# Two-layer mLSTM/HGRN2 encoder: the order of a few matmul pairs early in some weight-stationary chunks

## The chip, the cores and the metric

The kernel runs on one core of a Trainium2 chip. The metric is the device time of one execution in microseconds (us), as the median of several runs. All data is float32. Large products are made from two float32r parts of each factor, a high and a low one, of which three of the four cross products are kept.

## The reference, cut to what matters

The program is a trunk of two layers over 256 tokens of width 2048. Layer 0 mixes tokens with a bidirectional mLSTM, layer 1 with a bidirectional HGRN2. Each mixer is followed by a gated MLP with a convolution of width 3 (ConvGLU, inner width 5504), and a last norm closes it.

```python
D_MODEL = 2048; SEQ = 256; DEPTH = 2; D_FF = 5504

def conv_glu(hn, w_up, conv_w, conv_b, w_down):
    u = hn @ w_up
    a, v = jnp.split(u, 2, axis=-1)
    ...
    return (jax.nn.gelu(c, approximate=False) * v) @ w_down

def reference(...):
    ...
    h = x
    for layer in range(DEPTH):
        hn = rmsnorm(h, norm_mix_g[layer])
        mix = mlstm_mixer(...) if layer % 2 == 0 else hgrn_mixer(...)
        h = h + mix
        h = h + conv_glu(rmsnorm(h, norm_ffn_g[layer]), ffn_w_up[layer], ...)
    return rmsnorm(h, final_g)
```

Nearly all of the time goes into products of the 256 tokens with the weights: `mlstm_w_in`, `mlstm_w_out`, `hgrn_w_in`, `hgrn_w_out`, and in each layer `ffn_w_up` (2048 x 11008) and `ffn_w_down` (5504 x 2048). Each weight is read once, 447 MB in all.

## The kernel before, in words

**Chunks.** All products with weights are cut into chunks (class `Chunk`), which the function `stream` runs through in one long list. There are two main kinds.

- A chunk of kind "tm" keeps tiles of x stationary and streams 512 columns of weights. For each of the inner blocks k of 128 rows and each half t of the tokens it issues three products of 512 columns (lines 192 to 194): x high by weights high, x high by weights low, x low by weights high.
- A chunk of kind "fm" keeps 128 columns of weights stationary and streams the tokens. It has 256 output features, in two halves f. For each k (16 of them) and each f it issues a *pair*: the **high** product (line 202), the weights' high part by x high and x low side by side, 512 columns; and the **low** product (line 209), the weights' low part by x high alone, 256 columns. Both add into one PSUM bank, `ps[f]`. So an fm chunk is 32 pairs, in the order high, low, high, low. Pairs are counted from 0 in the code: pair 2k + f.

(A third kind, "first", is used once at the start.)

**Weights.** `split_weights` fetches the raw weights in pieces of 1 MB on the SyncE queue, and for every 1024 columns ScalarE casts the high part (`wh`, line 147) and VectorE subtracts to get the low part (`wl`, line 148). `LOOK = 3` such pieces are made ahead. For an fm chunk one piece holds four k, that is eight pairs.

**The list.** The mLSTM gives, for each of four pairs of heads, a v chunk (tm; for the first it is the "first" chunk), a q chunk and a k chunk (fm) and an o chunk (tm); then four output chunks (tm). HGRN2 gives, for each of four groups `qd` of heads, three fm chunks (i = 0, 1, 2), a v chunk (tm), three fm chunks (i = 3, 4, 5) and a g chunk (tm); then four output chunks (tm). Each ConvGLU runs in two parts, of 22 and 21 feature blocks: 22 fm chunks up and four tm chunks down, then 21 fm chunks up and four tm chunks down. So an fm chunk follows a tm chunk at each q chunk from the second on, at i = 0 and i = 3 of each group of HGRN2, and at the first up chunk of each part.

**Side work.** What else a layer does (attention heads, norms, transposes) is written as generators, which `side.tick` advances while the products are being issued; their TensorE instructions thus come to stand between pairs. The tile framework then schedules all instructions by its own estimate of times, so that the order on an engine can differ from the order in the text.

**Dummy transposes.** An fm chunk can have `turns`: behind the high product of pair 1 (k = 0, f = 1) it issues so many transposes of the identity into an auxiliary PSUM tile named `turns` (lines 203 to 206). Nothing reads the result. The second, third and fourth q chunk have 1, 2 and 2, and the first up chunk of the second part in each layer has 1: seven transposes in all.

Of the kernel before, what the change touches and what calls it, by code (L numbers as in the profile page):

```python
# [15 lines left out]
P = 128  # L16
T = 256
D = 2048
KT = D // P
# [36 lines left out]
def trunk_kernel(ctx, tc, xT, x_d, fg_d, pp_d, cst_d, w_first, w_aq, w_ak, w_av, w_ao, w_aout,  # L56
# [24 lines left out]
    def aux(name):  # L81
        return psa.tile([P, 512], F32, tag="aux", name=name)


    class Side:
        def __init__(self):
            self.now, self.jobs = 0.0, []
# [25 lines left out]
    side = Side()  # L113


    class Chunk:
        def __init__(self, kind, src, nk, x, done, before=None, last=False, turns=0):
            self.last, self.turns = last, turns
            self.kind, self.src, self.nk, self.x, self.done, self.before = kind, src, nk, x, done, before
            self.width = {"fm": 256, "tm": 512, "first": 512 + P}[kind]  # L120

# [30 lines left out]
    def stream(chunks):  # L152
        pieces = split_weights(chunks)
        ready = []

        def fetch():
            p = next(pieces, None)
            if p is not None:
                ready.append(p)

        for _ in range(LOOK):
            fetch()
        for ch in chunks:
            if ch.before:
                ch.before()
            ps = [psm.tile([P, 512], F32, tag="mm", name="mm") for _ in range(3 if ch.kind == "first" else 2)]
            k = 0
            while k < ch.nk:
                fetch()
                wh, wl, n = ready.pop(0)  # L170
                if ch.last and k + sum(p[2] for p in ready) + n == ch.nk:
                    pieces_, k0 = [(wh, wl, n)] + ready, k
                    for t in range(2):
                        k = k0
                        for wh, wl, n in pieces_:
                            for kk in range(n):
                                x, c = ch.x(k), slice(kk * 512, (kk + 1) * 512)
                                xh, xl = x[:, t * P:(t + 1) * P], x[:, T + t * P:T + (t + 1) * P]
                                pe.matmul(ps[t], xh, wh[:, c], start=False, stop=False)
                                pe.matmul(ps[t], xh, wl[:, c], start=False, stop=False)  # L180
                                pe.matmul(ps[t], xl, wh[:, c], start=False, stop=k == ch.nk - 1)
                                k += 1
                        ch.half(ps[t], t)
                    return
                for kk in range(n):
                    x = ch.x(k)
                    st, sp = k == 0, k == ch.nk - 1
                    if ch.kind != "fm":
                        c = slice(kk * 512, (kk + 1) * 512)
                        for t in range(2):  # L190
                            xh, xl = x[:, t * P:(t + 1) * P], x[:, T + t * P:T + (t + 1) * P]
                            pe.matmul(ps[t], xh, wh[:, c], start=st, stop=False)  # L192
                            pe.matmul(ps[t], xh, wl[:, c], start=False, stop=False)  # L193
                            pe.matmul(ps[t], xl, wh[:, c], start=False, stop=sp)  # L194
                        if ch.kind == "first":
                            pe.matmul(ps[2], wh[:, 512:512 + P], x, start=st, stop=False)
                            pe.matmul(ps[2][:, 0:T], wl[:, 512:512 + P], x[:, 0:T], start=False, stop=sp)
                        side.tick(1.3)
                    else:
                        for f in range(len(ps)):  # L200
                            c = kk * ch.width + f * P
                            pe.matmul(ps[f], wh[:, c:c + P], x, start=st, stop=False)  # L202
                            if f and k == 0 and ch.turns:
                                it = aux("turns")
                                for i in range(ch.turns):
                                    pe.transpose(it[:, i * P:(i + 1) * P], ident, ident)
                            if f:
                                side.tick(0.325 * len(ps))
                            pe.matmul(ps[f][:, 0:T], wl[:, c:c + P], x[:, 0:T], start=False, stop=sp)  # L209
                    k += 1  # L210
            ch.done(ps)

# [179 lines left out]
    def mlstm(norm, nxt):  # L392
# [151 lines left out]
        for pr in range(AH // 2):  # L544
            st = dict(pr=pr, y=[None, None], W=[None, None])

            def done_v(ps, st=st):
                Vh = box["mp"].tile([P, 2, 2, 258], F32R, tag="Vh", bufs=1, name="Vh")
                Vl = box["mp"].tile([P, 2, 2, 258], F32R, tag="Vl", bufs=1, name="Vl")
                for t in range(2):  # L550
                    act.copy(Vh[:, t, :, 256:258], pad[:, 0:4].rearrange("p (a b) -> p a b", a=2))
                    act.copy(Vl[:, t, :, 256:258], pad[:, 4:8].rearrange("p (a b) -> p a b", a=2))
                    v, sc = ps[t].rearrange("p (a b) -> p a b", a=2), norm.rc[:, t:t + 1]
                    act.activation(Vh[:, t, :, 0:256], v, AF.Copy, scale=sc)
                    dve.scalar_tensor_tensor(Vl[:, t, :, 0:256], v, sc, Vh[:, t, :, 0:256].bitcast(F32),
                                             ALU.mult, ALU.subtract)
                st["V"] = (Vh, Vl)

            def done_q(ps, st=st):
                st["q"] = [box["mp"].tile([P, T], F32, tag="q", bufs=2, name="q") for _ in range(2)]  # L560
                for j in range(2):
                    fm_scaled(ps[j], norm.R, st["q"][j], QSCALE)
                for j in range(2):
                    st["W"][j] = weights(2 * st["pr"] + j)

            def done_k(ps, st=st):
                st["k"] = [box["mp"].tile([P, T], F32, tag="k", bufs=2, name="k") for _ in range(2)]
                for j in range(2):
                    fm_scaled(ps[j], norm.R, st["k"][j])
                    side.push(head(st, j))  # L570

            def done_o(ps, st=st):
                sg = box["mp"].tile([P, 2, 512], F32, tag="sg", bufs=1, name="sg")
                for t in range(2):
                    act.activation(sg[:, t], ps[t], AF.Sigmoid, scale=norm.rc[:, t:t + 1])
                st["sg"] = sg
                side.push(finish(st))

            def done_first(ps, done_v=done_v):
                done_v(ps[0:2])  # L580
                gates(ps[2])
                for t in range(2):
                    pool.dma_start(hm[:, t], x_d[t])

            if pr == 0:
                chunks.append(Chunk("first", w_first, KT, first_x, done_first, begin))
            else:
                chunks.append(Chunk("tm", w_av[pr - 1], KT, norm.x, done_v))
            chunks.append(Chunk("fm", w_aq[pr], KT, norm.x, done_q, turns=(0, 1, 2, 2)[pr]))
            chunks.append(Chunk("fm", w_ak[pr], KT, norm.x, done_k))  # L590
            chunks.append(Chunk("tm", w_ao[pr], KT, norm.x, done_o))

# [13 lines left out]
    def hgrn(norm, nxt):  # L606
# [166 lines left out]
        for qd in range(BH // 4):  # L773
# [14 lines left out]
            for i in range(6):  # L788
                if i == 3:
                    chunks.append(Chunk("tm", w_bv[qd], KT, norm.x, done_v))  # L790
                def done_i(ps, i=i, qd=qd):
                    for f in range(2):
                        r = 2 * i + f
                        take(4 * qd + r // 3, r % 3, ps[f])
                chunks.append(Chunk("fm", w_bq[6 * qd + i], KT, norm.x, done_i, begin if not chunks else None))
            for j in range(4):
                heads[4 * qd + j]["qd"] = four
            chunks.append(Chunk("tm", w_bg[qd], KT, norm.x, done_g))
# [14 lines left out]
    def ffn(layer, norm, nxt):  # L813
# [30 lines left out]
        for part, (f0, nf) in enumerate(((0, FA), (FA, FB))):  # L844
            GT = []
            for i in range(nf):
                chunks.append(Chunk("fm", w_up[layer, f0 + i], KT, norm.x, done_up(f0 + i, i, GT),
                                    begin if f0 + i == 0 else None,
                                    turns=1 if part and i == 0 else 0))
            chunks += project(lambda c: w_down[layer, c][:, f0 * 512:(f0 + nf) * 512], nf,  # L850
                              lambda k, GT=GT: GT[k], nxt if part else None)
        return chunks, stack.close
# [108 lines left out]
```

## Time and profile before

| | |
|---|---|
| median of 3 runs | 2440.34 us (2439.63 to 2445.22) |
| the profiled execution | 2440.68 us, its span 2438.6 us |
| mean granted TensorE clock in it | 0.998 |
| VectorE, ScalarE, GpSimdE busy | 69%, 50%, 7% |
| memory read | 447.35 MB, 184 GB/s over the span |
| high products L202, low products L209 | 3776 each |
| products of the down and output projections and v, o, g chunks | 390 to 396 ns each by their groups |

The page lists groups of instructions as line, engine, operation, tiles out<-in, shapes, count, then busy time and mean duration in ns, then the idle time in front of them and what ended it. Matmuls overlap: a product's duration is longer than the distance to the next one's start, so paces are read from starts and counts, not from durations. In the timeline the columns are start and duration in us, engine, line and operation; equal neighbours are merged with their count. A window's row gives its length, each engine's busy time with the number of instructions, the granted clock, the DMA share and GB/s. In the trace of before, stretches are these (us from the start of the span):

| stretch | us |
|---|---|
| second, third, fourth q and k chunk of the mLSTM | 112.7 to 135, 185.7 to 208, 258.9 to 282 |
| layer 0, up part 1 and up part 2 | 400.5 to 646.0, 765.7 to 1003.3 |
| HGRN2, fm and tm chunks up to its output projection | 1120.4 to 1593 |
| layer 1, up part 1 and up part 2 | 1712.4 to 1958.0, 2077.7 to 2315.2 |

### The profile page before, as it was taken

Reading aid. Unit: us, or ns where it says so; the run is one execution under the profiler, and the core shown is the slowest. Engines: PE = TensorE matmul, PEld = TensorE weight load, DVE = VectorE, ACT = ScalarE, POOL = GpSimd, SP = SyncE. Lnnn points to the kernel's source line nnn. Section 1 sums busy time; section 2 is a strip of 40 time slices with the busy share of each in tenths; the row PEclk is TensorE's granted clock in tenths of the full one; section 3 lists DMA queues with packets and bytes.
Section 4 is the critical chain, followed back from the end, with each engine's and each line's share of the span. In section 5 each row is a group of like instructions: output and inputs, shape, how many; then the busy total and the mean of one; then the engine's idle time right before and its main releaser. Section 6 shows DMA issues by size and latency. Waiting matters only on the chain.

```text
span 2438.6 us, 37099 instructions
## 1 busy us (share of the span) xinstructions
PE 2422.2 (99%) x14767; PEld 2068.0 (85%) x14767; DVE 1692.7 (69%) x2768; ACT 1208.0 (50%) x1831; POOL 160.9 (7%) x219
## 2 busy tenths in 40 slices
PE   9999999999999999999999999999999999999998
PEld 7888888888888888888888888888888888888887
DVE  7766556777645777657887988885677754677754
ACT  6655455444434444445554555545544443444443
POOL 0100000000000000001222222220000000000000
PEclk9999999999999999999999999999999999999999
DMA  7654555555555555555544554455555555555554
GB/s 288 199 180 160 186 177 186 190 190 190 191 197 184 188 190 186 183 192 184 173 163 167 173 172 159 172 178 194 183 190 190 190 193 197 185 185 188 190 185 143
DMA packets 66205, 451.90 MB, mean 185 GB/s; under 512 B 7648, under 2 KB 8160, under 8 KB 13424
## 3 DMA queue, kind: packets, MB, share of 16 engines
q1 hardware_dynamic: 63792, 442.91, 53.4%
q0 software_dynamic: 1232, 5.31, 0.9%
q8 instruction: 115, 1.88, 0.3%
q10 hardware_dynamic: 1008, 1.32, 0.2%
q14 instruction: 58, 0.48, 0.1%
HBM read 447.35 MB, written 2.16 MB: 184 GB/s over the span
## 4 chain that ended last, share of the span: by engine, by line
PE 97%; DVE 1%; issue 1%; ACT 0%; DMA 0%; SPq 0%; POOLq 0%; POOL 0%; ACTq 0%
PE mm L202 36%; PE mm L209 18%; PE mm L192 13%; PE mm L194 13%; PE mm L193 13%; PE pn L508 1%; PE pd L694 1%; PE py L746 1%; PE pz L276 0%; DVE wl L148 0%; PE S L494 0%; PE pa L694 0%; DMA raw<-in_w_first 0%; PE pa L720 0%; DVE QK L706 0%
## 5 line engine op out<-in xcount | busy, mean ns | idle before, releaser
L148 DVE TENSOR_TENSOR wl<-raw,wh 128x1024 fp32r<-128x1024 f32 (+1 forms) x848 | 1032.2, 1219 | 594.3 <-ACT wh L147 584.1
L202 PE MATMUL mm<-xt,wh 128*128 128x512 f32 x3776 | 1326.6, 396 | 0.0
L147 ACT CAST wh<-raw 128x1024 fp32r<-128x1024 f32 (+1 forms) x848 | 881.2, 1041 | 879.0 <-PE mm L194 401.6
L209 PE MATMUL mm<-xt,wl 128*128 128x256 f32 x3776 | 1058.1, 280 | 1.8 <-issue 1.8
L202 PEld LDWEIGHTS mm<-xt,wh 128*128 128x128 f32 x3776 | 709.1, 188 | 167.9 <-issue 2.0
L209 PEld LDWEIGHTS mm<-xt,wl 128*128 128x128 f32 x3776 | 712.5, 189 | 2.1
L194 PE MATMUL mm<-wh,g 128*128 128x512 f32 x674 | 262.8, 390 | 0.0
L192 PE MATMUL mm<-wh,g 128*128 128x512 f32 x674 | 262.6, 390 | 0.0
L193 PE MATMUL mm<-wl,g 128*128 128x512 f32 x674 | 262.3, 389 | 0.0
L192 PE MATMUL mm<-wh,xt 128*128 128x512 f32 x512 | 201.2, 396 | 2.7 <-ACT xt L214 2.2
L193 PE MATMUL mm<-wl,xt 128*128 128x512 f32 x512 | 200.9, 392 | 0.4 <-DVE wl L148 0.4
L194 PE MATMUL mm<-wh,xt 128*128 128x512 f32 x512 | 199.9, 392 | 0.0
L219 ACT COPY b<-mm 128x256 f32<-128x256 f32 x237 | 87.8, 370 | 175.4 <-PE mm L209 175.4
L194 PEld LDWEIGHTS mm<-wh,g 128*128 128x128 f32 x674 | 126.5, 188 | 26.6
L193 PEld LDWEIGHTS mm<-wl,g 128*128 128x128 f32 x674 | 126.5, 188 | 26.2
L192 PEld LDWEIGHTS mm<-wh,g 128*128 128x128 f32 x674 | 126.5, 188 | 26.1
L192 PEld LDWEIGHTS mm<-wh,xt 128*128 128x128 f32 x512 | 95.6, 188 | 23.1 <-ACT xt L214 2.9
L193 PEld LDWEIGHTS mm<-wl,xt 128*128 128x128 f32 x512 | 96.5, 188 | 20.0 <-DVE wl L148 0.8
L194 PEld LDWEIGHTS mm<-wh,xt 128*128 128x128 f32 x512 | 96.4, 188 | 19.8
L220 DVE TENSOR_TENSOR a<-mm,b 128x256 f32<-128x256 f32 x86 | 36.5, 425 | 54.3 <-ACT b L219 54.3
L686 DVE COPY kq<-QK 128x256 f32<-128x256 f32 x224 | 70.9, 337 | 0.0
L712 POOL TENSOR_TENSOR G<-G 128x384 f32<-128x384 f32 (+2 forms) x96 | 67.8, 707 | 6.3
(204 smaller groups left out, 1825.4 us busy)
## 6 DMA issues: line engine op xcount, KB each, us to landing
raw<-in_w_up SPq DMA_DIRECT2D x172, 1024.0 KB, 5.0
raw<-in_w_down SPq DMA_DIRECT2D x80, 1024.0 KB, 4.8
raw<-in_w_bq SPq DMA_DIRECT2D x48, 1024.0 KB, 5.0
raw<-in_w_ao SPq DMA_DIRECT2D x16, 1024.0 KB, 4.8
raw<-in_w_aout SPq DMA_DIRECT2D x16, 1024.0 KB, 4.8
raw<-in_w_bv SPq DMA_DIRECT2D x16, 1024.0 KB, 4.8
raw<-in_w_bg SPq DMA_DIRECT2D x16, 1024.0 KB, 4.8
raw<-in_w_bout SPq DMA_DIRECT2D x16, 1024.0 KB, 4.8
```

The lines of the kernel that those rows point to most:

```text
L147: act.copy(wh[:, :m], r)
L148: dve.tensor_tensor(wl[:, :m], r, wh[:, :m].bitcast(F32), ALU.subtract)
L192: pe.matmul(ps[t], xh, wh[:, c], start=st, stop=False)
L193: pe.matmul(ps[t], xh, wl[:, c], start=False, stop=False)
L194: pe.matmul(ps[t], xl, wh[:, c], start=False, stop=sp)
L202: pe.matmul(ps[f], wh[:, c:c + P], x, start=st, stop=False)
L209: pe.matmul(ps[f][:, 0:T], wl[:, c:c + P], x[:, 0:T], start=False, stop=sp)
L219: act.copy(b, ps[:, T:2 * T])
L220: dve.tensor_tensor(dst, ps[:, 0:T], b, ALU.add)
L508: pe.matmul(pn[:, 0:258], w, v, start=(i == 0), stop=(i == len(parts) - 1))
L686: dve.tensor_copy(m[:, j].rearrange("k (m p j) -> k m p j", p=2, j=h), blocks(z, h, 0, T))
L712: pool.tensor_tensor(G2, G[:, 0:6 * n:2], G[:, 1:6 * n:2], ALU.mult)
```

## The change

The dummy transposes and the argument `turns` go. A chunk gets the argument `swap` instead, a tuple of places. For an fm chunk the products of a piece are first written as a list, high and low by turns, and for each place i in `swap` (in the chunk's first piece alone) the low product of pair i and the high product of pair i + 1 are exchanged, so that the two pairs run as high, high, low, low. With i = 1 these are the pairs (k = 0, f = 1) and (k = 1, f = 0), with i = 2 the pairs (k = 1, f = 0) and (k = 1, f = 1). The sums are the same, each bank still starting with its own first high product and ending with its own last low one.

The places are: 2, 1 and 2 in the second, third and fourth q chunk; 2 in the chunk i = 0 of the second to fourth group of HGRN2 and 1 in the chunk i = 3 of all four; 2 in the first up chunk of the second part of layer 0 and 1 in that of layer 1. That is twelve swaps. The branches for fm and the other kinds are separated; the products of the other kinds are unchanged, and the advance of side work per k is the same 0.65.

```diff
-        def __init__(self, kind, src, nk, x, done, before=None, last=False, turns=0):
-            self.last, self.turns = last, turns
+        def __init__(self, kind, src, nk, x, done, before=None, last=False, swap=()):
+            self.last, self.swap = last, swap
...
+                if ch.kind == "fm":
+                    ops = [(kk, f, part) for kk in range(n) for f in range(2) for part in "hl"]
+                    for i in ch.swap if k == 0 else ():
+                        ops[2 * i + 1:2 * i + 3] = ops[2 * i + 2], ops[2 * i + 1]
+                    for kk, f, part in ops:
+                        x = ch.x(k + kk)
+                        c = kk * ch.width + f * P
+                        if part == "h":
+                            pe.matmul(ps[f], wh[:, c:c + P], x, start=k + kk == 0, stop=False)
+                            continue
+                        if f:
+                            side.tick(0.65)
+                        pe.matmul(ps[f][:, 0:T], wl[:, c:c + P], x[:, 0:T], start=False, stop=k + kk == ch.nk - 1)
+                    k += n
+                    continue
...
-                        for f in range(len(ps)):
-                            c = kk * ch.width + f * P
-                            pe.matmul(ps[f], wh[:, c:c + P], x, start=st, stop=False)
-                            if f and k == 0 and ch.turns:
-                                it = aux("turns")
-                                for i in range(ch.turns):
-                                    pe.transpose(it[:, i * P:(i + 1) * P], ident, ident)
-                            if f:
-                                side.tick(0.325 * len(ps))
-                            pe.matmul(ps[f][:, 0:T], wl[:, c:c + P], x[:, 0:T], start=False, stop=sp)
...
-            chunks.append(Chunk("fm", w_aq[pr], KT, norm.x, done_q, turns=(0, 1, 2, 2)[pr]))
+            chunks.append(Chunk("fm", w_aq[pr], KT, norm.x, done_q, swap=((), (2,), (1,), (2,))[pr]))
...
-                chunks.append(Chunk("fm", w_bq[6 * qd + i], KT, norm.x, done_i, begin if not chunks else None))
+                chunks.append(Chunk("fm", w_bq[6 * qd + i], KT, norm.x, done_i, begin if not chunks else None,
+                                    swap=(2,) if i == 0 and qd else (1,) if i == 3 else ()))
...
-                                    turns=1 if part and i == 0 else 0))
+                                    swap=(1 + (layer == 0),) if part and i == 0 else ()))
```

More of the change, by code (lines that the diff above doesn't have):

```diff
@@ L187, in stream @@
                     st, sp = k == 0, k == ch.nk - 1
[L188 to L199, printed above, removed]
-                        for f in range(len(ps)):
-                            c = kk * ch.width + f * P
-                            pe.matmul(ps[f], wh[:, c:c + P], x, start=st, stop=False)
-                            if f and k == 0 and ch.turns:
-                                it = aux("turns")
-                                for i in range(ch.turns):
-                                    pe.transpose(it[:, i * P:(i + 1) * P], ident, ident)
-                            if f:
-                                side.tick(0.325 * len(ps))
-                            pe.matmul(ps[f][:, 0:T], wl[:, c:c + P], x[:, 0:T], start=False, stop=sp)
+                    c = slice(kk * 512, (kk + 1) * 512)
+                    for t in range(2):
+                        xh, xl = x[:, t * P:(t + 1) * P], x[:, T + t * P:T + (t + 1) * P]
+                        pe.matmul(ps[t], xh, wh[:, c], start=st, stop=False)
+                        pe.matmul(ps[t], xh, wl[:, c], start=False, stop=False)
+                        pe.matmul(ps[t], xl, wh[:, c], start=False, stop=sp)
+                    if ch.kind == "first":
+                        pe.matmul(ps[2], wh[:, 512:512 + P], x, start=st, stop=False)
+                        pe.matmul(ps[2][:, 0:T], wl[:, 512:512 + P], x[:, 0:T], start=False, stop=sp)
+                    side.tick(1.3)
                     k += 1
```

## The prediction

> **What bounds the kernel now.** I read four views: the page's totals, the groups of TensorE products, the counts of products in equal windows, and the timeline of single products around the places that the change touches.
>
> ```profile
> PE 2422.2 (99%) x14767; PEld 2068.0 (85%) x14767; DVE 1692.7 (69%) x2768; ACT 1208.0 (50%) x1831; POOL 160.9 (7%) x219
> ...
> PE 97%; DVE 1%; issue 1%; ACT 0%; DMA 0%; SPq 0%; POOLq 0%; POOL 0%; ACTq 0%
> ...
> L202 PE MATMUL mm<-xt,wh 128*128 128x512 f32 x3776 | 1326.6, 396 | 0.0
> ...
> L209 PE MATMUL mm<-xt,wl 128*128 128x256 f32 x3776 | 1058.1, 280 | 1.8 <-issue 1.8
> ```
>
> TensorE is busy for 99% of the span and is 97% of the chain that ended last. The two lines of the fm chunks (high L202, low L209) are more than half of the chain, and the idle time in front of them is 0.0 and 1.8 us. So no other engine and no transfer sets the pace: a gain can only come from TensorE taking the same products at a shorter spacing, or from fewer of them. The spacing is what I looked at next, in four windows of 192 us, all inside up-projections: first and second part of layer 0, first and second part of layer 1.
>
> ```profile
> 450.00:642.00 192.00, 192.00 (x555) 1.00 0.57 192
> 780.00:972.00 192.00, 192.00 (x545) 1.00 0.56 187
> 1760.00:1952.00 192.00, 192.00 (x555) 1.00 0.57 189
> 2100.00:2292.00 192.00, 192.00 (x545) 1.00 0.56 186
> ```
>
> These count L202 alone: us, busy, count, granted clock, DMA share, GB/s. At the same full clock, with no idle TensorE and nothing that it waits for, the first parts get 555 high products through where the second parts get 545. The work of a pair is the same in all four. So the pair of high and low has **two paces**. The windows that hold the second to fourth q and k chunks of the mLSTM show the same two:
>
> ```profile
> 113.00:135.00 22.00, 21.93 (x64) 1.00 0.56 194
> 186.00:208.00 22.00, 21.82 (x64) 1.00 0.56 193
> 259.00:281.00 22.00, 21.82 (x62) 1.00 0.54 186
> ```
>
> The sizes of the paces come from single starts. In the slow stretch the starts of high products repeat every three pairs; six pairs take 801.87 - 799.75 = 2.12 us, 353.3 ns each. In the fast stretch 113.48 to 117.99 holds 13 pairs, 346.9 ns each; the windows agree (a product that overlaps an edge is counted, so (192 + 0.39)/555 = 346.6 and (192 + 0.40)/545 = 353.0). I use 346.7 and 353.3, a difference of **6.7 ns a pair, 1.9%**. The pace lasts: from 766.5 to 1003.3 all 670 pairs run slow, from 414.1 to 646.0 all 669 run fast. It changes only where something else stands between the products.
>
> ```profile
> 799.75 0.40 PE L202 MATMUL mm<-xt,wh 128*128 128x512 f32 x1
> ...
> 801.87 0.40 PE L202 MATMUL mm<-xt,wh 128*128 128x512 f32 x1
> ```
>
> **The change part by part.** *Dummy transposes removed.* There are seven: one, two and two in the second to fourth q chunk, and one at each second up part.
>
> ```profile
> 766.08 0.40 PE L202 MATMUL mm<-xt,wh 128*128 128x512 f32 x1
> 766.32 0.27 PE L206 MATMUL turns<-cst 128*128 128x128 f32 x1
> 766.35 0.36 PE L209 MATMUL mm<-xt,wl 128*128 128x256 f32 x1
> 766.55 0.39 PE L202 MATMUL mm<-xt,wh 128*128 128x512 f32 x1
> ```
>
> High to high takes 0.47 us here against 0.35, so one costs 0.12; with two it is 259.25 to 259.82, 0.57, so 0.22. Three places with one and two with two: 3 x 0.12 + 2 x 0.22 = **-0.8 us**. They lie on TensorE, the bound, and nothing waits for their result; the auxiliary PSUM buffer that they took is given back.
>
> *The order high, high, low, low, twelve times*: three q chunks, seven HGRN2 chunks (four at i = 3, three at i = 0), two up chunks. No instruction, transfer or wait is added. The scheduler has put the same order in by itself at 44.3 us:
>
> ```profile
> 44.00 0.39 PE L202 MATMUL mm<-xt,wh 128*128 128x512 f32 x1
> 44.23 0.28 PE L209 MATMUL mm<-xt,wl 128*128 128x256 f32 x1
> 44.34 0.63 PE L202 MATMUL mm<-xt,wh 128*128 128x512 f32 x2
> 44.81 0.40 PE L209 MATMUL mm<-xt,wl 128*128 128x256 f32 x2
> 45.05 0.40 PE L202 MATMUL mm<-xt,wh 128*128 128x512 f32 x1
> ```
>
> Three pairs in 45.05 - 44.00 = 1.05 us, against 3 x 346.7 = 1.04: 0.01 us each, **+0.1 us** for twelve. Below, it could give back the 0.01 by which two slow pairs are long; above, I bound it by a dummy transpose's 0.12, or 1.4 us for twelve. I take the same order's own row.
>
> [...]
>
> *What the order does to the pace* is the disputed part, since the trace has no such order in a slow stretch. It has near rows. The order stands once as written, at 44.3, and twice as high, high, low, high, low, low, at 413.1 and 1725.0; the pace behind all three is fast, but it was fast ahead of them too. Behind those last two, 669 pairs stay fast without a break, so the state that it leaves is at least a lasting one. Of twenty other interruptions of a slow stretch that I followed (groups of transposes, of py, pa and pd products), eleven left a fast stretch and nine a slow one; the block of eight py products did so each of six times (as at 1198.6, 1242.9 and 1326.2), while the dummy transposes, at this very spot, left a fast stretch at two of five places. Every fm chunk that follows products with x stationary enters slow when it is left alone (400.5, 1120.4, 1179.1 and seven more). So the twelve places are where a slow stretch begins, and a disturbance there has better than even odds. Three of three fast behind this order itself raises it; I take fast.
>
> With fast: two second up parts, 670 pairs each, 2 x 670 x 6.7 ns = **-9.0 us**; the fourth q and k chunks, 62 pairs, **-0.4**; in HGRN2 the seven swapped chunks have 7 to 10 slow pairs before the next interruption, some 7 of them behind the swap, 7 x 7 x 6.7 ns = **-0.3**, and what follows is set by those interruptions anyway (156 slow pairs there: if all go too, -1.4; +0.5 if half as many fast pairs go). The second and third q and k chunks are fast already: 0, but +0.8 (124 pairs) if the order fails there now that the transposes are gone.
>
> What could eat this: a faster part asks its weights sooner. The first parts do the same work per chunk at the fast pace with 57% DMA share, and no wait of TensorE is named in either stretch. So nothing is late next.
>
> **Sum**: -0.8 + 0.1 - 9.0 - 0.4 - 0.3 = -10.4 on the profiled execution's 2440.7 (span 2438.6 and 2.1 around it), which is 0.3 above the median of 2440.3 and so stands for it. Forecast **2430.3**.
>
> **One cost outside the change** widens it. In this execution TensorE stood still once, in HGRN2:
>
> ```profile
> 1318.58 0.28 PE L209 MATMUL mm<-xt,wl 128*128 128x256 f32 x1 [1.79 <-issue]
> ```
>
> ```profile
> 1320.00:1322.00 2.00, 2.00 (x8) 0.50 0.03 8
> ```
>
> The product ahead began at 1316.39, so the gap is 2.19 us where 0.24 is usual: 1.95 lost, with no releaser shown. Then the granted clock (third figure of the window: 0.69, 0.50 and 0.95 in the windows from 1318 to 1324) costs 2 x (0.31 + 0.50 + 0.05) = 1.7. The like places at 1191.9, 1382.0 and 1443.6 have no such gap. If it is missing in the changed kernel, 3.6 us go; if there are two, 3.6 come.
>
> **The rivals.** *1. The order leaves the pace as it is.* The same products and loads, so the same two paces; or the scheduler, which made its own order at 44.3, issues another than is written. For it: at 44.3 the pace was the same ahead and behind, and the transposes failed at three of five places. Against it: the slow pace gives way to eleven of twenty interruptions. Time: 2440.7 - 0.8 + 0.1 = 2440.0, or 2440.8 if the second and third q and k chunks fall slow.
>
> [...] The trace does not agree that the rate is a matter of the products alone: 346.7 and 353.3 ns for identical pairs.
>
> *2. Only one up part turns fast.* The two are swapped at different places (at pairs 2 and 3, counted from 0, in layer 0; at 1 and 2 in layer 1), and the slow starts repeat every three pairs, so the order meets them in different phases. Against: both enter alike, 0.226 or 0.227 us to the first low and 0.113 or 0.114 to the next high. Time: 2430.3 + 4.5 = 2434.8, and up to 0.8 more with a q chunk failing.
>
> *3. Slower: the first up parts lose their pace.* They hold no swap. They start slow and turn fast at 409.9 and 1721.9, behind other products that the scheduler sets between them from its own reckoning of times; an interrupted fast stretch is not always fast behind it (two transposes at 1268.1 left a slow one). If the shorter code ahead shifts that placing, both can run slow for 669 pairs: 2 x 4.5 = +9.0. It decides once the second parts do not turn fast: 2440.0 + 9.0 = 2449.0; with them fast the two cancel and the time is 2439.3. Against: both layers got the same placing and the same end, at very different times.
>
> **How the numbers follow.** Forecast 0.55; rival 1 0.20; rival 2 0.17; rival 3 0.08. The likeliest is 2430.3, its own range 2426.5 (without the gap at 1318, 3.6 less, rounded) to 2433 (the swaps' upper price, 1.3 more, and the upper bound of HGRN2, 0.8 more, with half a microsecond for the runs' spread). For 8 in 10 the range reaches over rivals 2 and 1: **2426.5 to 2441**, leaving out rival 3 with both parts slow and a second gap. A change under 0.3%, 7.3 us, is about what a measurement of this kernel cannot tell from none, so faster means below 2433.0: nearly all of the forecast's 0.55, and of rival 2 the part in which the gap also goes, 0.03: **0.57**. Slower is above 2447.7: rival 3 without its cancelling, and rival 1 with two more gaps: **0.08**. The rest, **0.35**, is the same.
>
> **What would show it.** Right: windows of 192 us inside the second up parts count 555 of the high products, and pairs behind the swap come at 346.7 ns. The seven transposes are gone, and the third and fourth q chunks start with no 0.22 us extra. Wrong: 545 in one window (rival 2) or both (rival 1); 545 in a first part (rival 3); a pair group high, high, low, low that takes over 0.75 us (its price); a wait in front of the low products. The forecast falls if the order and the pace turn out unrelated, whatever the sign.

## The result, and the profile after

The changed kernel takes 2431.91 us (median of 5, 2431.55 to 2433.88), the kernel before beside it 2440.53. The ratio is 0.9965, 95% interval 0.9954 to 0.9976. The forecast was 2430.3, range 2426.5 to 2441. The profiled execution is 2431.91 us, span 2429.9, against 2440.68 and 2438.6.

The page's totals of the changed kernel: busy time of the engines, and the chain that ended last, by engine and by line (L193 is the high product of an fm pair now, L197 the low one, L206 to L208 the tm products).

```profile
PE 2411.1 (99%) x14760; PEld 2062.3 (85%) x14760; DVE 1692.1 (70%) x2768; ACT 1207.8 (50%) x1831; POOL 160.9 (7%) x219
...
PE 98%; DVE 1%; issue 1%; DMA 0%; ACT 0%; SPq 0%; POOLq 0%; POOL 0%; ACTq 0%
PE mm L193 36%; PE mm L197 18%; PE mm L206 13%; PE mm L207 13%; PE mm L208 13%; PE pn L511 1%; PE pd L697 1%; PE py L749 1%; PE pz L279 0%; DVE wl L148 0%; PE S L497 0%; PE pa L697 0%; DMA raw<-in_w_first 0%; PE pa L723 0%; DVE QK L709 0%
```

TensorE still sets the end, with seven products fewer (14760 against 14767) and 11.1 us less busy time. The view that carried the prediction, the high products in equal windows (us, busy, count, granted clock, DMA share, GB/s):

```profile
450.00:642.00 192.00, 192.00 (x555) 1.00 0.56 191
780.00:972.00 192.00, 192.00 (x555) 1.00 0.56 192
1760.00:1952.00 192.00, 192.00 (x555) 1.00 0.56 189
2100.00:2292.00 192.00, 192.00 (x555) 1.00 0.56 191
113.00:135.00 22.00, 21.93 (x64) 1.00 0.55 195
186.00:208.00 22.00, 21.93 (x64) 1.00 0.55 196
259.00:281.00 22.00, 21.89 (x64) 1.00 0.56 194
```

The two counts of 545 have become 555, and the 62 of the fourth q and k chunk 64. The timeline at the swap of the second up part of layer 1 shows the order as written, two highs and two lows merged to x2:

```profile
2073.59 0.39 PE L193 MATMUL mm<-xt,wh 128*128 128x512 f32 x1
2073.82 0.28 PE L197 MATMUL mm<-xt,wl 128*128 128x256 f32 x1
2073.93 0.63 PE L193 MATMUL mm<-xt,wh 128*128 128x512 f32 x2
2074.40 0.39 PE L197 MATMUL mm<-xt,wl 128*128 128x256 f32 x2
2074.63 0.40 PE L193 MATMUL mm<-xt,wh 128*128 128x512 f32 x1
```

From 2073.93 to 2074.63 two pairs take 0.70 us, and behind them all 669 pairs keep 346.7 ns. By starts in the traces, stage by stage:

| stage | before | after | difference |
|---|---|---|---|
| start to the second q chunk | 112.7 | 112.9 | +0.2 |
| second, third, fourth q and k chunk | 22.30, 22.41, 22.82 | 22.20, 22.19, 22.20 | -0.9 |
| second up part, layers 0 and 1 | 237.53, 237.53 | 232.98, 232.96 | -9.1 |
| HGRN2 to its output projection | 1120.4 to 1593.0 | 1115.0 to 1588.8 | +1.2 |

So what the change was about gave 10.0 us, and HGRN2 took back 1.2. Where, the view of TensorE's waits says (who waited for whom, us in total, times, longest). First two lines of before, then three of the changed kernel:

```profile
PE mm L209 <- issue: 1.8, 1, 1.8
PE pd L694 <- issue: 1.3, 1, 1.3
```

```profile
PE pd L697 <- issue: 3.2, 3, 1.5
...
PE mm L193 <- issue: 2.1, 1, 2.1
...
PE mm L197 <- DVE q L230: 1.0, 1, 1.0
```

Before there was one such wait of 1.8 us (the low product near 1318) and one of 1.3 (pd, near 1486). After there are four places (gaps) where TensorE starts nothing for 1.4 to 2.3 us: near 1292, 1313, 1480 and 1501. The third line of after names VectorE, but that gap is of the same family, as the runs below show. The first of them in the timeline of the changed kernel:

```profile
1291.58 0.89 PE L697 MATMUL pd<-kq 128*32 128x32 f32 x79
1293.96 0.19 PE L697 MATMUL pd<-kq 128*32 128x32 f32 x1 [1.49 <-issue]
```

It stands inside HGRN2's dense block of small products, 144 of them with 144 weight loads per head.

### The profile page after: what moved, and what is told of

Same layout as the page of the kernel before. It is cut to its first block, busy times and chain, and to the rows that moved or that the text cites. A ratio compares the mean times of both kernels' runs of the same rounds, so it can differ in the third digit from the quotient of the medians.

```text
span 2429.9 us, 37085 instructions
## 1 busy us (share of the span) xinstructions
PE 2411.1 (99%) x14760; PEld 2062.3 (85%) x14760; DVE 1692.1 (70%) x2768; ACT 1207.8 (50%) x1831; POOL 160.9 (7%) x219
## 3 DMA queue, kind: packets, MB, share of 16 engines
q8 instruction: 115, 1.88, 0.3%
## 4 chain that ended last, share of the span: by engine, by line
PE 98%; DVE 1%; issue 1%; DMA 0%; ACT 0%; SPq 0%; POOLq 0%; POOL 0%; ACTq 0%
PE mm L193 36%; PE mm L197 18%; PE mm L206 13%; PE mm L207 13%; PE mm L208 13%; PE pn L511 1%; PE pd L697 1%; PE py L749 1%; PE pz L279 0%; DVE wl L148 0%; PE S L497 0%; PE pa L697 0%; DMA raw<-in_w_first 0%; PE pa L723 0%; DVE QK L709 0%
## 5 line engine op out<-in xcount | busy, mean ns | idle before, releaser
L193 PE MATMUL mm<-xt,wh 128*128 128x512 f32 x3776 | 1314.4, 394 | 2.1 <-issue 2.1
L197 PE MATMUL mm<-xt,wl 128*128 128x256 f32 x3776 | 1049.1, 279 | 1.0 <-DVE q L230 1.0
L193 PEld LDWEIGHTS mm<-xt,wh 128*128 128x128 f32 x3776 | 707.0, 188 | 161.3 <-issue 1.2
L197 PEld LDWEIGHTS mm<-xt,wl 128*128 128x128 f32 x3776 | 709.8, 188 | 5.2 <-issue 2.1
L208 PE MATMUL mm<-wh,g 128*128 128x512 f32 x674 | 262.8, 390 | 0.0
L206 PE MATMUL mm<-wh,g 128*128 128x512 f32 x674 | 262.5, 389 | 0.0
L206 PE MATMUL mm<-wh,xt 128*128 128x512 f32 x512 | 201.5, 397 | 2.5 <-ACT xt L217 2.5
L208 PE MATMUL mm<-wh,xt 128*128 128x512 f32 x512 | 200.3, 392 | 0.0
L206 PEld LDWEIGHTS mm<-wh,g 128*128 128x128 f32 x674 | 126.6, 188 | 26.5
L208 PEld LDWEIGHTS mm<-wh,g 128*128 128x128 f32 x674 | 126.5, 188 | 26.0
L206 PEld LDWEIGHTS mm<-wh,xt 128*128 128x128 f32 x512 | 95.9, 189 | 22.8 <-ACT xt L217 3.2
L208 PEld LDWEIGHTS mm<-wh,xt 128*128 128x128 f32 x512 | 96.6, 189 | 19.8
```

Source lines behind the costliest of these rows:

```text
L193: pe.matmul(ps[f], wh[:, c:c + P], x, start=k + kk == 0, stop=False)
```

## The experiments

Two questions were open: does the order set the pace, and by what rule; and what are the gaps in HGRN2. Each edit is against the changed kernel unless another is named; of a long line only the argument that changes is shown.

**Neither transposes nor swaps.**

```diff
-swap=((), (2,), (1,), (2,))[pr]
+swap=()
...
-swap=(2,) if i == 0 and qd else (1,) if i == 3 else ()
+swap=()
...
-swap=(1 + (layer == 0),) if part and i == 0 else ()
+swap=()
```

> Neither dummy transposes nor a swapped pair anywhere. Theory (the order high, high, low, low sets the pace): all twelve places stay at 353.3 ns a pair: both second up parts 670 pairs x 6.7 ns = 4.5 us longer each than in the changed kernel, the second to fourth q and k chunks 0.4 us longer each, so 9.0 + 1.2 + 0.3 = 10.5 us above the changed kernel's 2431.9, about 2442.4. Rival (it was the removal of the transposes, which had disturbed the pace): the second up parts run at 346.7 ns without any swap, and the time is 2431 to 2433.

Measured: 2443.99 us (2442.44 to 2445.3), ratio to the kernel before 1.0011 [1.0001, 1.0021]; 12.1 above the changed kernel. The second up parts, high products per window:

```profile
780.00:972.00 192.00, 192.00 (x545) 1.00 0.56 187
2100.00:2292.00 192.00, 192.00 (x544) 1.00 0.56 186
```

Each part takes 237.43 us, each q and k chunk pair 22.60, both 353.3 ns a pair. Left alone, every one of these entries runs long; it is the order that makes them short, not the transposes' going. The 1.6 us beyond the expected 10.5 lie in HGRN2 (476.3 us against 473.8), where some stretches behind other products also ran at 353.3 and the granted clock was at half for 3.4 us behind the gap at 1507, which cost 1.7.

**Other places for the same order.**

```diff
-swap=((), (2,), (1,), (2,))[pr]
+swap=((), (3,), (4,), (6,))[pr]
...
-swap=(2,) if i == 0 and qd else (1,) if i == 3 else ()
+swap={0: ((), (1,), (3,), (4,)), 3: ((2,), (3,), (4,), (5,))}[i][qd] if i % 3 == 0 else ()
...
-swap=(1 + (layer == 0),) if part and i == 0 else ()
+swap=(1 if layer == 0 else 3,) if part and i == 0 else ()
```

> The same order at other pairs: places 1 to 6 instead of 1 and 2, another one than before at each of the twelve chunks. Theory (the order leaves the short pace wherever it stands): 346.7 ns a pair behind all twelve, time within 1 us of 2431.9 but for stalls. Rival (the phase of the three-pair rhythm decides): places that are 0, 1 or 2 modulo 3 differ, and about a third to two thirds of the twelve stay at 353.3; if both up parts do, the time is 2441.

Measured: 2438.81 us (one execution). The windows: the second up parts (place 1 in layer 0, place 3 in layer 1), then the q and k chunks with places 3, 4 and 6.

```profile
780.00:972.00 192.00, 192.00 (x555) 1.00 0.58 192
2100.00:2292.00 192.00, 192.00 (x544) 1.00 0.56 186
115.00:135.00 20.00, 20.00 (x57) 1.00 0.54 186
189.00:208.00 19.00, 19.00 (x56) 1.00 0.57 196
262.00:281.00 19.00, 19.00 (x55) 1.00 0.57 191
```

The three chunk pairs last 22.60, 22.20 and 22.60 us. Places 3 and 6 stay at 353.3; 1 and 4 go to 346.7; in HGRN2, where only a few pairs follow, places 1, 2, 4 and 5 leave 347 to 348 and place 3 351 to 353. The rival was right: the three-pair rhythm decides. **A swap in a slow stretch works where its place is not a multiple of three**, and it did the same in every chunk in which a place was tried. Place 0 was not tried; place 5 rests on three pairs of one chunk, place 6 on one chunk. The changed kernel uses only 1 and 2, both good.

**Other orders at the same chunks.** LLHH is high, low, low, high; NEST is high, high, low, high, low, low; THREE is three highs, three lows.

```diff
-                        ops[2 * i + 1:2 * i + 3] = ops[2 * i + 2], ops[2 * i + 1]
+                        ops[2 * i:2 * i + len(how)] = [ops[2 * i + j] for j in how]
...
+    LLHH = (0, 1, 3, 2)
+    NEST = (0, 2, 1, 4, 3, 5)
+    THREE = (0, 2, 4, 1, 3, 5)
...
```

> Other orders of the same products at the same twelve chunks: low before high in one pair (high, low, low, high), three pairs as high, high, low, high, low, low, and three as high, high, high, low, low, low. Theory (two low products in a row, with two loads behind short products, reset the pace): all three orders contain that and all twelve chunks run at 346.7 behind them. Rival (two high products in a row with nothing between them do it, by giving the loads time to get ahead): the first order has its two highs behind the two lows and the others ahead, so that kinds of order part into short and long paces. A further rival is that any result can come, by phase, about half and half.

Measured: 2434.69 us (one execution). LLHH with pair 2 turned round: 346.7 in the second up part of layer 0 (232.98 us); with pair 3: 353.3 (22.60 for the third q and k chunk). NEST at 1: 353.3 (22.59). THREE at 1 and at 2: 346.7 (232.97 and 22.22). Each kind holds two lows in a row, so "two lows reset the pace" falls, and so does "two highs". What is left is the further rival: any of these orders may do it, and kind and place together decide. Why a given one does is not shown.

**Price and reach.**

```diff
-swap=(1 + (layer == 0),) if part and i == 0 else ()
+swap=((1,) if i == 0 else ()) if not part else ((1, 4) if i else (2,)) if layer == 0 else (2,) if i == 10 else ()
```

> Price and reach of the order. In the second up part of layer 0 each of the 20 later chunks has two more swaps, 40 in all; in that of layer 1 the first swap stands in the eleventh chunk only; the first up chunk of both layers' first part has one at place 1. Theory: 40 swaps at 0.012 us make the part 0.5 us longer than in the changed kernel (233.0 us), at 346.7 between them; in layer 1 ten chunks run at 353.3 and the rest at 346.7, so the part takes 320 x 6.7 ns = 2.1 us more. Rival (each swap draws the next state by chance): some swaps in layer 0 end in 353.3 and the part is 2 to 4 us longer; a swap far from the chunk's start does nothing in layer 1, which takes 4.5 us more.

Measured: 2434.89 us (one execution). Forty further swaps made the part 233.51 us against 232.98: 13 ns each, and every stretch between them kept 346.7, at places of every phase. In layer 1 the high products ahead of and behind the one swap in the eleventh chunk, in windows of 80 us:

```profile
2100.00:2180.00 80.00, 80.00 (x228) 1.00 0.57 186
2200.00:2280.00 80.00, 80.00 (x232) 1.00 0.56 186
```

The part takes 235.10 us, 2.1 more, as the theory had it. The swap stands at pair 322, which is 1 modulo 3; the short pace, once reached, stays. The swap at place 1 shortens each first up part from 245.53 to 245.45 us.

**A steady rhythm of the order.** In the second up parts every two pairs (layer 0) or four pairs (layer 1) run highs first, then lows.

```diff
+                    if ch.run:
+                        m = ch.run
+                        ops = [ops[j + 2 * p + b] for j in range(0, len(ops), 2 * m) for b in range(2) for p in range(m)]
...
-swap=(1 + (layer == 0),) if part and i == 0 else ()
+run=(2, 4)[layer] if part else 0
```

> The second up part of layer 0 runs all its pairs as high, high, low, low, that of layer 1 as four highs and then four lows; the rest as changed. If the order high, high, low, low costs its 0.012 us each time, the part in layer 0 takes 336 x 12 ns = 4 us more than 233.0; if the price is only that of leaving the rhythm, it stays at 346.7 a pair, 233.0. For the four lows: a load behind each short product; at the 117 ns that two lows are apart it is 233.0 too; if the loads run short at the 1.5 times that the longest record of one, 188 ns, would give, it takes 10 us or more on top.

Measured: 2431.60 us (one execution); the parts take 234.07 and 235.73 us. In layer 1 (L196 high, L200 low here):

```profile
2099.97 1.09 PE L196 MATMUL mm<-xt,wh 128*128 128x512 f32 x4
2100.90 0.63 PE L200 MATMUL mm<-xt,wl 128*128 128x256 f32 x4
2101.37 1.09 PE L196 MATMUL mm<-xt,wh 128*128 128x512 f32 x4
```

Four pairs take 2101.37 - 2099.97 = 1.40 us, 350 ns each, between the two paces. The price of twos is 1.1 us over 336, 3 ns each, a quarter of the isolated swap's; neither steady order is better than the usual one at its short pace. Nothing here ran below 346.7 a pair.

This run also bears on the gaps. Its time is no longer than the changed kernel's, though its parts take 3.9 us more, because HGRN2 takes 469.4 us instead of 473.8. The products there are the same, but TensorE's stream holds 39 more semaphore instructions ahead of HGRN2 (67 against 28 in the trace), and the four gaps are not there: three others are, near 1497, 1542 and 1618.

**The stream shifted by twelve instructions**, as the transposes had it: three more idle products at the start.

```diff
-    for _ in range(8):
+    for _ in range(11):
         pe.matmul(idle[:, 0:P], ones[:, 0:P], ones[:, 0:P], start=True, stop=True)
```

> The changed kernel with three more of the idle products at the very start: twelve TensorE instructions, in a place where TensorE waits over 2 us for its first data, so that every later instruction stands twelve places further on in the stream, as it stood before the change. Theory (the shortfall of 1.4 us against the forecast comes from TensorE's instruction stream, which arrives in pieces of 256 instructions; the seven transposes' going has moved the pieces' ends against the dense blocks of small products in HGRN2): of the four gaps of over 1.3 us in HGRN2 two vanish, near 1291 and 1500, as in the kernel before, and the time is about 2430.4. Rival (the gaps are chance or follow from the earlier arrival at HGRN2): four gaps stay at the same places and the time is 2431.9.

Measured: the profiled execution has two gaps, near 1311 and 1479, as the theory had it, and took 2429.03 us. But seven executions spread from 2429.03 to 2437.77, median 2432.51 and not the 2430.4 of the theory, ratio 0.9964 [0.9951, 0.9978]. The kernel before, whose blocks stand at the same place in the stream, spread about as widely beside it (2439.18 to 2446.68). That the gaps differ from one execution to the next is likely from this; only one of the seven has a trace.

**The block parted.** Two points at which pairs of the running chunk may come in between.

```diff
+            yield 0.1
             for i in reversed(range(FINE)):
+                if i == 1:
+                    yield 0.1
                 product(pd[:, (i + 1) * 64:(i + 2) * 64], *ms[i], QUAD, lambda b: b * QUAD)
```

> The changed kernel; HGRN2's block of small products per head gets two points at which pairs of the running chunk may come between (in some heads the scheduler joins the block again). Theory (the block uses up 288 instructions faster than the next 256 arrive): the gaps at 1313 and 1501, which stand behind blocks that are now parted, shrink or go, those at 1292 and 1480, whose blocks stay whole, remain; time 2429 to 2431. Rival (the gap depends on the stream's place alone): all four remain, time 2431.9 or a little more for the further interruptions.

Measured: 2434.96 us (2433.97 to 2435.98), ratio 0.9971 [0.9961, 0.9981], 3.1 above the changed kernel; in the traces HGRN2 takes 476.7 us against 473.8. The gaps went as the theory had it: the one near 1313 is gone, those near 1292 and 1480 stay, the one at 1501 is shorter (1.84 us, at 1504). But parting costs 0.5 to 0.7 us in each stretch without a gap. A miss as a remedy.

**Twelve instructions and more swaps** in HGRN2.

```diff
-    for _ in range(8):
+    for _ in range(11):
...
-swap=(2,) if i == 0 and qd else (1,) if i == 3 else ()
+swap=(2,) if i == 0 and qd else (1,) if i in (1, 3, 4) else ()
```

> As the run with three more idle products, with a further swap at place 1 in the chunks i = 1 and i = 4 of HGRN2, where some stretches of 19 pairs run at 353.3. Theory: 2430.4 less 0.1 to 0.4, no more than a median can tell; in the trace the stretch near 1187 and its like run at 346.7 where their phase is right (two of three). Rival: the swaps disturb what follows as often as they help, 2430.4 to 2430.8.

Measured: 2431.88 us (2427.89 to 2435.80), ratio 0.9956 [0.994, 0.9971]. The profiled execution had three gaps, one of 3.1 us; the spread hides anything of 0.4 us, so the time says nothing. In the trace the swaps did what was meant: behind them 12 pairs run at 347 ns in six of seven stretches (the seventh lies at half clock), and the stretch near 1187, at 352 ahead of its swap, is one of the six.

**The stream shifted by 196**, and the changed kernel again beside it.

```diff
+    for _ in range(49):
+        pe.matmul(idle[0:QUAD, 0:4], ones[:, 0:QUAD], ones[:, 0:4], start=True, stop=True)
     for _ in range(8):
```

> The changed kernel with 49 tiny idle products (32 x 4) at the very start, 196 TensorE instructions, mostly inside the 2.1 us in which TensorE waits for its first data. Theory (where a gap falls is set by where a dense block of 288 instructions stands against the stream's pieces of 256): blocks that begin at 141 to 198 modulo 256 had gaps so far; shifted by 196 these are the blocks that began near 1246 and 1435 in the changed kernel, with 1227 and 1291 at the margins. So the gaps near 1292, 1313, 1480 and 1501 go and up to two or three come, near 1246 and 1435; HGRN2 is 2 to 4 us shorter, the time 2428 to 2430. Rival (the gaps belong to these heads and the transfers beside them): four gaps at 1292, 1313, 1480 and 1501 as before, 2432 or, with the added products, 2433.

> The changed kernel as it is, for the spread on the same chip as the run above. Theory: four gaps at 1292, 1313, 1480 and 1501 once more, median 2431.5 to 2432.5, and the same paces behind all twelve swaps. Rival (the gaps are chance): other places or another number, and a spread of several us between executions.

Measured: shifted 2426.16 us (2425.97 to 2426.36), ratio 0.9938 [0.9925, 0.995]; as it is 2433.28 (2431.84 to 2434.28), ratio 0.9966 [0.9952, 0.9979], above the 2431.5 to 2432.5 that was expected, with its four gaps at 1292, 1313, 1480 and 1501 once more, one of 1.0 us at 1623, and 3.4 us at half clock from 1504.9 on, which the first profile did not have. TensorE's busy time over HGRN2, first as changed (the first profile), then shifted:

```profile
1115.00:1589.00 474.00, 468.00 (x4375) 1.00 0.49 170
```

```profile
1120.00:1590.00 470.00, 469.67 (x4377) 1.00 0.51 171
```

6.0 us idle against 0.3. The shifted kernel's view of TensorE's waits is down to two lines:

```profile
PE idle L865 <- POOL ones L859: 1.1, 1, 1.1
PE pd L697 <- issue: 0.3, 1, 0.3
```

The four gaps are gone, none came near 1435, and near 1249 one of 0.3 us is left; five executions lie within 0.4 us.

That the gaps follow the place of the instructions in the stream is shown, and more sharply than I had it. Count in each trace the weight loads, products and semaphore instructions of TensorE that stand ahead of the one that comes late. In eleven of the fourteen traces there are 38 gaps of over 0.7 us from start to start behind the first 20 us (the other three have none), and at each of them this count is 192 or 193 modulo 256: in the steady run too, where 39 semaphore instructions had moved the gaps, and also at the 0.3 us left here. So every gap stands at one and the same point of the count modulo 256. Where a block must stand for a gap to come there is known less well: my window of 141 to 198 modulo 256 for the block's begin is not the whole rule, since of two blocks at 167 and 169 one now has 0.3 us and the other nothing. What else a long gap needs (a transfer in the way at that moment, for one) stays open.

**The kernel before, shifted to the same place**: 46 such tiny products, 184 instructions, against the kernel before.

> The kernel before, with its transposes and without swaps, with 46 tiny idle products at the start, 184 instructions, which put its blocks in HGRN2 where those of the run shifted by 196 stand. What the change is worth with no gap in either kernel. Theory: none of the gaps, and above that run's 2426.2 by what the paces and transposes cost alone: 9.1 in the second up parts, 0.9 in the q and k chunks, 0.2 in HGRN2, so 2436.4, a ratio of 0.9958 the other way round. Rival (the gaps depend on the order of products too): gaps in HGRN2 and 2438 to 2441.

Measured: 2436.09 us (2435.64 to 2436.35), ratio to the kernel before 0.9971 [0.996, 0.9982], no gap of over 0.2 us. So with both kernels clear of gaps the change is worth 2436.09 - 2426.16 = **9.9 us**. The two were measured on different chips; the next run, on the same chip as this one, took 2425.77, which is 10.3 less, and some 0.4 of that belong to its other places.

**Shifted, with the best places seen.**

```diff
-swap=(2,) if i == 0 and qd else (1,) if i == 3 else ()
+swap=(1,) if i == 0 and qd else (4,) if i == 3 else ()
...
-swap=(1 + (layer == 0),) if part and i == 0 else ()
+swap=(1,) if i == 0 else ()
```

(with the 49 tiny products)

> The run shifted by 196 with other places: 1 at i = 0 and 4 at i = 3 in HGRN2 (the places of the earlier run behind which the least was left at 353.3), 1 in all four first up chunks, those of the first parts too. Theory: 0.08 less in each first part, 0.1 in each of the four i = 3 stretches, 0.04 in each of three at i = 0: 0.7 less than 2426.2, 2425.5. Rival: the interruptions in HGRN2 draw other results and the time is 2426.0 to 2426.5.

Measured: 2425.77 us (2425.35 to 2426.11), ratio 0.9929 [0.9917, 0.9942]. The first up parts took 245.45 us against 245.53, two i = 3 stretches 37.19 against 37.26, one i = 0 stretch 39.22 against 39.40, the other stretches within 0.04; that is about 0.5, the medians differ by 0.4, of the expected 0.7. The ratio's interval overlaps that of the run shifted by 196, so this gain rests on the stretches alone. It beats both kernels.

## Why the prediction was right, and where it was off

*What bounds the kernel, and its two paces*: right. TensorE sets the end, and 346.7 and 353.3 ns are the only two paces of the ordinary order in every long stretch.

*Second up parts, -9.0, and their two transposes, -0.24*: measured -9.1. *The fourth q and k chunks, -0.4, and the transposes of three q chunks, -0.56*: measured -0.9. *The swap's own price, 0.012 us*: 13 ns by forty of them.

*Why the order turns the pace*: the outcome was right, the argument weak. I counted odds over interruptions (eleven of twenty) and took the three fast rows at 44.3, 413.1 and 1725.0 as support, though a fast stretch ahead of them could show nothing of a slow one. For a swap there are no odds: the slow rhythm has a period of three pairs (in the trace of before the starts of its high products are 349, 350, 361 ns apart, over and over; in the fast one 350 and 343), and the same place did the same each time. I named that phase in rival 2, and gave it 0.17 as a chance of one part failing; its mechanism was real, and only the places chosen here, 1 and 2, made it harmless. That both are good was luck as far as the prediction goes. A place of 3 in layer 1 cost 4.5 us, as rival 2 had it. For other interruptions there are odds still. Two transposes at one and the same place left the third q and k chunks fast and the fourth slow in before (22.41 and 22.82 us), and the other way round in the shifted before (22.82 and 22.41). Behind the dense block near 1186 the changed kernel ran 19 pairs at 353.3 in one profile and at 346.9 in the other. What in TensorE makes the two rhythms no run shows, nor whether a short delay at the same place, without another order, would do what the swap does.

*The ground of rival 1, the same products and loads and so the same two paces*: it does not agree with the traces. The kernel without swaps and the changed one issue the same products in second up parts that take 237.4 and 233.0 us.

*HGRN2, -0.3*: measured +1.2. This is the term that was mis-sized, and with it the sentence that the transposes' going costs nothing beside its 0.8. The swaps' own gain there was 0.06 us in each of three i = 3 stretches and nothing at i = 0, where the eight py products behind the swap now left 353.3 in place of 346.7. The rest is the gaps. I had found one, saw no releaser, and priced it as chance, 3.6 us up or down; the waits of before already held a second, 1.3 us on a pd product, that I left out. Six of the seven transposes stand ahead of HGRN2; without them and their loads the dense blocks stand twelve places earlier in the stream, and two gaps became four. TensorE's busy time over HGRN2 in before:

```profile
1120.00:1593.00 473.00, 469.87 (x4376) 1.00 0.50 170
```

That is 3.1 us idle, against 6.0 after: 2.9 more. The 1.7 us that before lost at half clock behind its gap at 1318 did not come in this profile of the changed kernel, which leaves the 1.2. They came in its second profile, where HGRN2 took 3.4 us more than in before; that the first was spared them was chance. The forecast time is 1.6 us too low, nearly all of it by this one term. Without gaps the sum of the other terms holds: -10.4 forecast, -9.9 measured.

*Rivals 1 and 3* did not come: no first part lost its pace, in any of the runs.

## What to carry to other kernels

Where one engine is busy for 99%, count its instructions in equal windows over stretches of equal work: two counts (here 555 and 545 in 192 us) point to two rhythms, and a rhythm that repeats over several instructions may be broken by one exchange, if the place fits its phase (here from 353.3 to 346.7 ns a pair, at places 1, 2 and 4 and not at 3 and 6). Before a small edit is judged by its median, see what it does to the place of all later instructions: a gap that no wait explains may belong to the stream and not to the edit (here all 38 gaps stood at 192 or 193 modulo 256). That is tested by shifting the stream where the engine is idle anyway, which here was worth 7.1 us (2433.28 to 2426.16) beside the change's 9.9, and by counting the instructions ahead of each gap.

## What the runs showed of the hardware that was not expected

The pair of a 512-column and a 256-column product had two stable rhythms at full clock in the usual order, 346.7 and 353.3 ns, that lasted over more than 660 pairs, across 21 chunks, until something else stood between or the order changed.

That TensorE's instructions arrive in pieces of 256 is my estimate from these numbers: in the changed kernel its 2 x 14760 products and loads (29520) stand against 115 transfers of the queue q8, of kind "instruction" on the page, 1.88 MB, 16 KB each, some 257 for each transfer; in up parts at the short pace such a transfer begins every 22.2 us, and in the second up parts of before every 22.6, which is at both paces 64 pairs or 256 instructions. In the changed kernel's DMA view of 1479 to 1482, around the third gap, that queue's piece is there:

```profile
q8 instruction: 1, 0.02, 1.8%
```

In all six gaps of the two profiles such a transfer ends 1.2 to 1.6 us ahead of TensorE's next start, and so it is in all 38 gaps counted above. At the short pace 256 instructions of the up parts take 22.2 us; a dense block's 288 take 1.9 (1313.94 to 1315.82 in before), and each of the six gaps stands in such a block or less than 2 us behind one. That TensorE waits there for its next piece is inferred, from the same count modulo 256 at every gap, from the time behind the transfer and from the shifts; the profile shows no such wait by name.
